# Scratch reads from another queue, polled searches, an earlier load of a norm weight and two new pacing rates in a two-block transformer kernel

## The chip, the cores and the metric

The kernel runs on one core of one Trainium2 chip. The metric is the device time of one execution in microseconds, the median of three runs. One profiled execution of the same kernel gives the rows below.

## What is computed

A 256-token sequence of width 2048 goes through two blocks. The first one mixes by convolution and neighbourhood attention and ends in an MLP; the second mixes by latent attention and a gated unit and ends in a layer of 16384 experts (PEER), of which every token uses 8 heads times 16 experts. The change lies wholly in that last layer:

```python
def peer_ffn(h, w_pq, peer_keys, peer_u, peer_v):
    q = jnp.einsum("bsd,dhk->bshk", h, w_pq).reshape(B, S, PEER_HEADS, 2, KEY_DIM)
    sub = jnp.einsum("bshpk,hpnk->bshpn", q, peer_keys).astype(jnp.float32)
    s, i = lax.top_k(sub, PEER_TOPK)
    cand = (s[..., 0, :, None] + s[..., 1, None, :]).reshape(B, S, PEER_HEADS, PEER_TOPK * PEER_TOPK)
    cidx = (i[..., 0, :, None] * N_KEYS + i[..., 1, None, :]).reshape(...)
    top_s, pos = lax.top_k(cand, PEER_TOPK)
    idx = jnp.take_along_axis(cidx, pos, axis=-1)
    gate = jax.nn.softmax(top_s, axis=-1).astype(h.dtype)
    ...
        u = jnp.take(peer_u, i_blk, axis=0)
        a = jax.nn.gelu(jnp.einsum("td,thkd->thk", x_blk, u)) * g_blk
        v = jnp.take(peer_v, i_blk, axis=0)
        return jnp.einsum("thk,thkd->td", a, v)
```

The kernel computes 192 of the 256 tokens densely: it multiplies them with all 16384 rows of `peer_u`, applies GELU, multiplies by a gate that is zero for the experts not chosen, and multiplies with all of `peer_v`. The other 64 tokens are done sparsely: only the chosen rows are gathered.

## The kernel before, in words

All large products go through one pipeline. A weight tile of 128x2048 floats (1 MB) is loaded by SyncE into one of three `raw` buffers; a piece is half of it, 128x1024. `prep` splits a piece into two roundings: ScalarE writes `whi` (L131), VectorE writes the remainder `wlo` (L132), and TensorE multiplies with both (L264). There are four `whi`/`wlo` pairs, and pieces are prepared up to three ahead (`LOOK = 3`). When the second half of a `raw` tile has been split, SyncE is given the load of the tile three further on (L209). SyncE's queue holds nothing else in this part.

All other work is written as generators. `tick` is called after each piece and advances each generator in the list by its rate: 1.0 means one step per piece, 0.45 means 0.45 steps per piece. A generator that is started in a piece skips the tick of that piece. `drain` runs a generator to its end at once, so that all that is left of it is put into the engines' queues in one burst. Engines work their queues in order, so the order in which the generators are stepped is the order of VectorE.

The stages of the last layer, with the generators of each:

- Query groups (four, eight pieces each). After group n `key_gen(n)` makes the scores `sub` in five steps, and `lists_gen(n)` (L1485 to L1489) polls until the scores are there and then makes eight searches, one per step: the 16 best of 128 scores for one head and half.
- `U0` to `U3`: passes over `peer_u`, each of four groups of eight pieces, so 32 pieces. After each group `turn(n)` transposes the result into a ring (GELU). `turn(8)` first drains `top_gen`.
- `top_gen` starts with the last query group. It drains all `key_gen` and `lists_gen`, then makes the best 16 of the 256 sums for each head (L1525 and again L1485 on 256 elements) and the gates. It has 57 steps after the waiting, at one per piece.
- `g_gen` (rate 0.5, 25 steps) follows it: it builds the dense gates with one-hot products and writes them to a DRAM scratch in 24 writes (L1690, GpSimd's queue). At its end it starts `sparse`.
- `r_gen(e)`, e from 0 to 7: after the last `turn` of U pass e, after `g_gen` and after `r_gen(e-1)`, it reads the gates of pass e back from the scratch in three reads of 512 KB (L1698, GpSimd's queue, one buffer `t`), and multiplies the ring with each (L1703, VectorE). In step j the read is issued; two ticks later comes the multiply.
- `sparse` (rate 0.45 in U passes, 0.28 in V passes, set by `pace`): the first step loads the norm's weight `g_n2` broadcast over 128 partitions (1 MB, GpSimd's queue), multiplies the 64 tokens with it (L1591) and copies the product to the other partitions (L1592, GpSimd's queue). The second issues three gathers (L1598, GpSimd's queue) and computes the first; each of the 128 steps gathers 128 rows (1 MB) into one of three buffers, and VectorE multiplies and reduces them (L1608, `peer_u`) or adds them up (L1610, `peer_v`).
- `V` passes over `peer_v`: 32 pieces each. Before each second piece `jit_V` splits two columns of the ring (`s_vj`), and before the first piece of a pass it drains `top_gen`, `g_gen` and the `r_gen` of that pass. `jit_V` runs two pieces ahead.

The order of passes is U0 U1 U2 U3 V0 U4 V1 U5 V2 U6 V3 U7 and then V4 to V7 as one pass of 128 pieces. In the trace U3 ends and V0 begins at 2302.7 us; U4 lies from 2401.5 to 2480.2, V1 to 2576.0, U5 to 2654.6, V2 to 2744.1, U6 to 2822.7, V3 to 2916.3, U7 to 2995.0, and the last pass to 3329.

Of the kernel before, what the change touches and what calls it, by code (L numbers as in the profile page):

```python
# [12 lines left out]
OP = mybir.AluOpType  # L13
# [925 lines left out]

GATE_RATE = 0.5  # L940

SPARSE_RATE = (0.45, 0.28)
CONV_RATE = [1.7, 1.2]
NA_RATE = [1.0, 1.0]
CONV_POOL = (2, 3, 6, 7)
# [2 lines left out]
def phase3(b, C, W, gs, X, ident, transposes, residual, norm_of, stat2, act_pair, lhs_of, res_need, bcast, jits,  # L948
# [546 lines left out]

    def lists_gen(n):
        V16, I16, _, rep = found()
        while not gs["key", n].done:
            yield
        for h in range(2):  # L1500
            for m in range(4 * n, 4 * n + 4):
                o = (h * 16 + m) * 16
                top16(V16[:, o:o + 16], I16[:, o:o + 16], SUB(h)[:, m * 128:m * 128 + 128], rep[m % 2][:, :128])
                yield

    def top_gen():
        V16, I16, If, rep = found()
        for n in range(4):
            gs["key", n].drain()
            gs["lists", n].drain()  # L1510
        V.tensor_copy(If, I16)
        yield
        t8 = H(8, "sub")
        T16 = t8[:, 0:128]
        Pi, Pa, Pb = (t8[:, k * 128:k * 128 + 128].bitcast(U32) for k in (1, 2, 3))
        Fa, Fb, E = t8[:, 512:640], t8[:, 640:768], t8[:, 768:1152]
        sm = t8[:, 1152:1160]
        cand, eq = H(16, "k")[:, :], H(17, "k")[:, :]
        i1, i2, g12, it2 = sarr16()
        V.tensor_copy(it2, iota[:, :, None].to_broadcast([128, 128, 2]))  # L1520
        for h in range(2):
            v4 = V16[:, h * 256:h * 256 + 256].rearrange("p (m q k) -> p m q k", m=8, q=2)
            f4 = If[:, h * 256:h * 256 + 256].rearrange("p (m q k) -> p m q k", m=8, q=2)
            for m in (0, 4):
                V.tensor_tensor(cand[:, m * 256:m * 256 + 1024].rearrange("p (m a c) -> p m a c", m=4, a=16),  # L1525
                                v4[:, m:m + 4, 0, :, None].to_broadcast([128, 4, 16, 16]),
                                v4[:, m:m + 4, 1, None, :].to_broadcast([128, 4, 16, 16]), op=OP.add)
                yield
            for m in range(8):
                top16(T16[:, m * 16:m * 16 + 16], Pi[:, m * 16:m * 16 + 16], cand[:, m * 256:m * 256 + 256],  # L1530
                      rep[m % 2])
                yield
            V.tensor_scalar(Pa, Pi, 4, None, op0=OP.logical_shift_right)
            V.tensor_scalar(Pb, Pi, 15, None, op0=OP.bitwise_and)
            V.tensor_copy(Fa, Pa)
            V.tensor_copy(Fb, Pb)
            yield
            for q, F in enumerate((Fa, Fb)):
                for m in (0, 4):
                    e1 = eq[:, m * 256:m * 256 + 1024]  # L1540
                    e3 = e1.rearrange("p (s a) -> p s a", a=16)
                    e4 = e1.rearrange("p (m s a) -> p m s a", m=4, s=16)
                    V.tensor_tensor(e3, F[:, m * 16:m * 16 + 64, None].to_broadcast([128, 64, 16]),
                                    iota[:, None, 0:16].to_broadcast([128, 64, 16]), op=OP.is_equal)
                    yield
                    V.tensor_tensor(e4, e4, f4[:, m:m + 4, q, None, :].to_broadcast([128, 4, 16, 16]), op=OP.mult)
                    yield
                    V.tensor_reduce(E[:, q * 128 + m * 16:q * 128 + m * 16 + 64], e3, axis=AX.X, op=OP.add)
                    yield
            g = E[:, 256:384].rearrange("p (m s) -> p m s", m=8)  # L1550
            t3 = T16.rearrange("p (m s) -> p m s", m=8)
            V.tensor_tensor(g, t3, t3[:, :, 0:1].to_broadcast([128, 8, 16]), op=OP.subtract)
            A.activation(g, g, AF.Exp)
            V.tensor_reduce(sm, g, axis=AX.X, op=OP.add)
            V.reciprocal(sm, sm)
            V.tensor_tensor(g, g, sm[:, :, None].to_broadcast([128, 8, 16]), op=OP.mult)
            if h:
                t = t8[:, 1160:1288].bitcast(I32)
                V.scalar_tensor_tensor(t, E[:, 0:128], 128.0, E[:, 128:256], op0=OP.mult, op1=OP.add)
                V.tensor_copy(which[64:128], t[64:128, 0:64])  # L1560
                V.tensor_copy(share[64:128], E[64:128, 256:320])
                nc.gpsimd.dma_start(which[0:64], t[64:128, 64:128])
                nc.gpsimd.dma_start(share[0:64], E[64:128, 320:384])
            for _ in range(4):
                yield
            p = b.bank()
            for k in range(3):
                PE.transpose(p[:, k * 128:k * 128 + 128], E[:, k * 128:k * 128 + 128], ident)
            s = slice(h * 128, h * 128 + 128)
            V.tensor_copy(i1[:, s], p[:, 0:128])  # L1570
            V.tensor_copy(i2[:, s], p[:, 128:256])
            V.tensor_scalar(g12[:, 0, s], p[:, 256:384], GSCALE, None, op0=OP.mult)
            V.scalar_tensor_tensor(g12[:, 1, s], p[:, 256:384], GSCALE, g12[:, 0, s], op0=OP.mult, op1=OP.subtract)
            yield
        gs["G"] = b.start(g_gen(), GATE_RATE)


# [6 lines left out]
    def sparse():  # L1584
        xs = H(8, "sp")[:, :]
        buf = [H(5, "gb")[:, :], H(16, "k")[:, :], H(17, "k")[:, :]]
        hi, lo = slice(64, 128), slice(0, 64)
        nc.gpsimd.dma_start(buf[2], bcast("g_n2"))
        A.activation(Y()[hi], X[1][hi], AF.Copy)
        G.memset(Y()[lo], 0.0)  # L1590
        V.tensor_tensor(xs[hi], X[1][hi], buf[2][hi], op=OP.mult)  # L1591
        nc.gpsimd.dma_start(xs[lo], xs[hi])  # L1592
        G.memset(X[1][hi], 0.0)
        yield

        def load(g):
            at = bass.IndirectOffsetOnAxis(ap=which[:, g % 64:g % 64 + 1], axis=0)
            nc.gpsimd.indirect_dma_start(buf[g % 3], None, d["v_rows" if g // 64 else "u_rows"], at)  # L1598

        def gelu(a, z):  # L1600
            A.activation(act[:, a:z], act[:, a:z], AF.Gelu_apprx_tanh, scale=rsp)
            V.tensor_tensor(act[:, a:z], act[:, a:z], share[:, a:z], op=OP.mult)
        for g in range(3):
            load(g)
        for g in range(128):
            t, a = buf[g % 3], act[:, g % 64:g % 64 + 1]
            if g < 64:
                V.tensor_tensor_reduce(t, t, xs, 1.0, 0.0, OP.mult, OP.add, a)  # L1608
            else:
                V.scalar_tensor_tensor(Y(), t, a, Y(), op0=OP.mult, op1=OP.add)  # L1610
            if g + 3 < 128:
                load(g + 3)
            if g in (32, 64):
                gelu(g - 32, g)
            yield
# [42 lines left out]
    def g_gen():  # L1658


        i1, i2, g12, it2 = sarr16()
        i1, i2, g1, g2 = (a.rearrange("p (k u t) -> p k u t", u=4, t=2) for a in (i1, i2, g12[:, 0], g12[:, 1]))
        numbers = it2[:, None, :, :].to_broadcast([128, 4, 128, 2])
        room = [H(5, "gb"), H(17, "k")]
        out = [H(16, "k")[:, i * 1024:i * 1024 + 1024] for i in range(2)]
# [27 lines left out]
    def r_gen(e):  # L1693
        while not (gs["s", 4 * e + 3].done and "G" in gs and gs["G"].done and (e == 0 or gs["R", e - 1].done)):
            yield
        t = H(7, "g")[:, 1024:2048]
        for j in range(3):
            nc.gpsimd.dma_start(t.rearrange("p (k m) -> p k m", k=8),  # L1698
                                b.scratch[8 * j:8 * j + 8, :, 128 * e:128 * e + 128].rearrange("k p m -> p k m"))
            yield  # L1700
            yield
            R = ring(e, j // 2)[:, :, j % 2 * 64:j % 2 * 64 + 64].rearrange("p n (k t) -> p k n t", k=8)
            V.tensor_tensor(R, R, t.rearrange("p (k n t) -> p k n t", k=8, n=16), op=OP.mult)  # L1703
            yield
# [32 lines left out]
    def post_V(last, g):  # L1737
        def f(p, halves=(0, 1), blocks=(0, 1)):
# [3 lines left out]
            for h in halves:  # L1742
                for k in blocks:
                    s = slice((2 * g + k) * 512, (2 * g + k) * 512 + 512)
                    V.tensor_tensor(X[h][:, s], X[h][:, s], b.ps[p.banks[h][k]][:, :], op=OP.add)  # L1745
                    if last and h == 0:
                        A.activation(b.bank()[:, :], X[h][:, s], AF.Square,  # L1747
                                     accum_out=ssf[:, h, 2 * g + k:2 * g + k + 1])
                    elif last and g:
                        gs["gain"].drain()  # L1750
                        join(2 * g + k)
            if last and g and 1 in blocks:
# [168 lines left out]
```

## Time and profile before

| | us |
|---|---|
| median of three runs | 3346.87 |
| lowest, highest | 3342.87, 3348.78 |
| the profiled execution, its own time | 3345.87 |
| span of its trace, first to last instruction | 3344.1 |
| TensorE busy | 3185.3 (95%) |
| VectorE busy | 2271.5 (68%) |
| ScalarE busy | 1728.1 (52%) |
| GpSimd busy | 505.3 (15%) |

Busy is the time in which an engine works an instruction. The granted clock is the share of TensorE's full clock (2.4 GHz) that it was allowed, so 0.5 is 1.2 GHz. The share of the DMA is the mean busy share of the core's 16 DMA engines.

### The profile page before, as it was taken

The numbers are of one execution on the slowest core, as the hardware profiler recorded it, in microseconds if no ns is written. First come the engines' busy times: TensorE is split into PE (matmuls) and PEld (weight loads), VectorE is DVE, ScalarE is ACT, GpSimd is POOL, SyncE is SP. The second block draws the span as 40 slices with busy tenths as digits, with TensorE's granted clock in tenths as the row PEclk, the third lists the DMA queues.
The fourth block names the chain that finished last, engine by engine and source line by source line (L and its number), as shares of the span: only waits on it lengthen the run. The fifth ranks groups of instructions, "written<-read, shape, count | busy, mean of one in ns | idle before, by whom it ended". The sixth has DMA issues, their size and how long they took to land. (4 is left out here: it accounts for less than half of the span.)

```text
span 3344.1 us, 37944 instructions
## 1 busy us (share of the span) xinstructions
PE 3185.3 (95%) x14264; PEld 2485.6 (74%) x14264; DVE 2271.5 (68%) x2847; ACT 1728.1 (52%) x2490; POOL 505.3 (15%) x397
## 2 busy tenths in 40 slices
PE   8899999999999999999999989997999989898998
PEld 6577778888888798877778867775676767675776
DVE  6995544444555656544555799867878888886885
ACT  5666454444454465455445445763454545454554
POOL 3861100000000100000002000013222222332210
PEclk9899999999999999999999999998999999998999
DMA  6444455555555455444455445778898989797984
GB/s 220 142 165 170 171 191 186 177 178 187 189 189 189 156 177 212 178 147 141 169 180 184 170 165 211 255 257 331 325 368 315 403 310 396 282 411 270 351 323 151
DMA packets 113736, 768.52 MB, mean 230 GB/s; under 512 B 13008, under 2 KB 13440, under 8 KB 26064
## 3 DMA queue, kind: packets, MB, share of 16 engines
q1 hardware_dynamic: 84960, 591.70, 48.7%
q0 software_dynamic: 28304, 173.36, 13.5%
q8 instruction: 111, 1.82, 0.2%
q10 hardware_dynamic: 288, 1.05, 0.1%
q14 instruction: 73, 0.60, 0.1%
HBM read 750.82 MB, written 14.68 MB: 229 GB/s over the span
## 5 line engine op out<-in xcount | busy, mean ns | idle before, releaser
L132 DVE TENSOR_TENSOR wlo<-raw,whi 128x1024 fp32r<-128x1024 f32 (+2 forms) x1101 | 1350.8, 1235 | 797.6 <-ACT whi L131 790.2
L131 ACT ACTIVATE whi<-raw 128x1024 fp32r<-128x1024 f32 (+2 forms) x1113 | 1168.4, 1053 | 1117.0 <-PE ps L264 956.0
L264 PE MATMUL ps<-whi,s_x 128*128 128x512 f32 (+2 forms) x2816 | 907.8, 398 | 11.7 <-ACT whi L131 6.3
L264 PEld LDWEIGHTS ps<-whi,s_x 128*128 128x128 f32 x2816 | 532.8, 190 | 138.1 <-issue 8.3
L264 PE MATMUL ps<-whi,s_h 128*128 128x512 f32 x1760 | 609.2, 403 | 0.0
L264 PE MATMUL ps<-whi,s_vj 128*128 128x512 f32 x1536 | 549.6, 413 | 28.2 <-DVE s_vj L132 24.9
L264 PE MATMUL ps<-wlo,s_x 128*128 128x512 f32 (+2 forms) x1408 | 555.4, 394 | 13.0 <-DVE wlo L132 13.0
L264 PE MATMUL ps<-wlo,s_h 128*128 128x512 f32 (+1 forms) x1136 | 454.3, 400 | 34.9 <-DVE wlo L132 34.9
L264 PE MATMUL ps<-wlo,s_vj 128*128 128x512 f32 (+1 forms) x1024 | 416.3, 407 | 40.1 <-DVE wlo L132 40.1
L264 PEld LDWEIGHTS ps<-whi,s_h 128*128 128x128 f32 x1760 | 334.9, 190 | 101.3 <-issue 1.4
L264 PEld LDWEIGHTS ps<-whi,s_vj 128*128 128x128 f32 x1536 | 299.2, 196 | 140.6 <-DVE s_vj L132 36.9
L264 PE MATMUL ps<-whi,s_fj 128*128 128x512 f32 x1024 | 324.4, 397 | 2.8 <-DVE s_fj L132 2.0
L264 PEld LDWEIGHTS ps<-wlo,s_x 128*128 128x128 f32 x1408 | 267.3, 190 | 77.3 <-DVE wlo L132 21.4
L264 PEld LDWEIGHTS ps<-wlo,s_h 128*128 128x128 f32 (+1 forms) x1136 | 187.9, 165 | 88.2 <-DVE wlo L132 41.2
L264 PEld LDWEIGHTS ps<-wlo,s_vj 128*128 128x128 f32 (+1 forms) x1024 | 170.9, 167 | 92.1 <-DVE wlo L132 44.7
L264 PEld LDWEIGHTS ps<-whi,s_fj 128*128 128x128 f32 x1024 | 193.5, 189 | 51.4 <-DVE s_fj L132 2.5
L264 PE MATMUL ps<-wlo,s_fj 128*128 128x512 f32 x512 | 203.6, 398 | 0.0
L132 POOL TENSOR_TENSOR s_head<-raw,s_head 128x1024 fp32r<-128x1024 f32 x6 | 17.5, 2932 | 896.0 <-ACT s_head L131 896.0
L517 POOL TENSOR_TENSOR s_conv<-s_conv,s_u 128x256 f32<-128x256 f32 x120 | 125.6, 1080 | 43.1 <-ACT s_u L516 42.8
L1598 POOL DMA_INDIRECT s_k<-in_v_rows,vec x43 | 81.6, 1897 | 244.4 <-DVE s_sp L1610 224.5
L264 PEld LDWEIGHTS ps<-wlo,s_fj 128*128 128x128 f32 x512 | 96.8, 189 | 22.7
L1598 POOL DMA_INDIRECT s_k<-in_u_rows,vec x42 | 69.9, 1664 | 214.5 <-DVE misc L1608 210.7
(335 smaller groups left out, 3039.3 us busy)
## 6 DMA issues: line engine op xcount, KB each, us to landing
raw<-in_peer_u SPq DMA_DIRECT2D x128, 1024.0 KB, 5.8
raw<-in_peer_v SPq DMA_DIRECT2D x128, 1024.0 KB, 6.8
raw<-in_w_in SPq DMA_DIRECT2D x101, 1024.0 KB, 4.8
raw<-in_w_up SPq DMA_DIRECT2D x64, 1024.0 KB, 4.8
raw<-in_w_down SPq DMA_DIRECT2D x64, 1024.0 KB, 4.8
raw<-in_w_out SPq DMA_DIRECT2D x32, 1024.0 KB, 4.8
raw<-in_w_pq SPq DMA_DIRECT2D x16, 1024.0 KB, 4.8
scratch<-s_k POOLq DMA_DIRECT2D x24, 512.0 KB, 3.8
```

The costliest lines, as they stand in the source:

```text
L131: nc.scalar.activation(hi, src, AF.Copy)
L132: (engine or nc.vector).tensor_tensor(lo, src, hi.bitcast(FT), op=OP.subtract)
L264: nc.tensor.matmul(self.ps[p.banks[h][b]][:xs[q].shape[-1], :w], xs[q], (wl if q == 1 else wh)[:, s], start=p.first and c == 0 and q == 0, ...
L517: G.tensor_tensor(o, o, t, op=OP.add)
L1598: nc.gpsimd.indirect_dma_start(buf[g % 3], None, d["v_rows" if g // 64 else "u_rows"], at)
```

## The change

The scratch reads of `r_gen` are issued by SyncE in place of GpSimd, and one more step lies between a read and its multiply. `lists_gen(n)` begins only after `lists_gen(n-1)` is done, and `top_gen` polls for the last of them instead of draining them. The load of `g_n2` moves from the start of `sparse` to the start of `g_gen`, into another buffer (`Y`); the copy in the setup of `sparse` goes to SyncE, the first three gathers are issued in its first step, and the clearing work forms a step of its own, so that the first gathered rows are used in the third step. The rates of `sparse` rise from 0.45 to 0.48 and from 0.28 to 0.30. The end of the last pass drains `sparse` before it drains the generator of the final gain.

```diff
-SPARSE_RATE = (0.45, 0.28)
+SPARSE_RATE = (0.48, 0.30)
...
-        while not gs["key", n].done:
+        while not (gs["key", n].done and (n == 0 or gs["lists", n - 1].done)):
             yield
...
-        for n in range(4):
-            gs["key", n].drain()
-            gs["lists", n].drain()
+        while not gs["lists", 3].done:
+            yield
         V.tensor_copy(If, I16)
...
-        nc.gpsimd.dma_start(buf[2], bcast("g_n2"))
-        A.activation(Y()[hi], X[1][hi], AF.Copy)
-        G.memset(Y()[lo], 0.0)
-        V.tensor_tensor(xs[hi], X[1][hi], buf[2][hi], op=OP.mult)
-        nc.gpsimd.dma_start(xs[lo], xs[hi])
-        G.memset(X[1][hi], 0.0)
-        yield
+        V.tensor_tensor(xs[hi], X[1][hi], Y()[hi], op=OP.mult)
+        nc.sync.dma_start(xs[lo], xs[hi])
...
         for g in range(3):
             load(g)
+        yield
+        A.activation(Y()[hi], X[1][hi], AF.Copy)
+        G.memset(Y()[lo], 0.0)
+        G.memset(X[1][hi], 0.0)
+        yield
...
+        nc.gpsimd.dma_start(Y(), bcast("g_n2"))
         numbers = it2[:, None, :, :].to_broadcast([128, 4, 128, 2])
...
-            nc.gpsimd.dma_start(t.rearrange("p (k m) -> p k m", k=8),
-                                b.scratch[8 * j:8 * j + 8, :, 128 * e:128 * e + 128].rearrange("k p m -> p k m"))
+            nc.sync.dma_start(t.rearrange("p (k m) -> p k m", k=8),
+                              b.scratch[8 * j:8 * j + 8, :, 128 * e:128 * e + 128].rearrange("k p m -> p k m"))
+            yield
             yield
             yield
...
+                        gs["sp"].drain()
                         gs["gain"].drain()
```

## Rows read from the trace of the kernel before

**Rows 1.** The page's part 1: busy time, share of the span, instructions of each engine.
```profile
PE 3185.3 (95%) x14264; PEld 2485.6 (74%) x14264; DVE 2271.5 (68%) x2847; ACT 1728.1 (52%) x2490; POOL 505.3 (15%) x397
```

**Rows 2.** Busy time by stretches: length, engines' busy us (instructions), clock, DMA share, GB/s.
```profile
1913.00:1970.00 57.00, 40.85 (x176) 29.76 (x175) 54.80 (x190) 20.74 (x24) 0.00 (x0) 0.88 0.32 111
2244.00:2302.70 58.70, 40.01 (x148) 28.59 (x148) 35.61 (x31) 16.88 (x21) 18.17 (x16) 0.85 0.81 302
2302.70:2401.50 98.80, 84.82 (x333) 61.12 (x332) 78.27 (x96) 42.90 (x67) 22.15 (x16) 0.91 0.86 320
2480.20:2576.00 95.80, 82.40 (x334) 60.72 (x333) 71.63 (x91) 43.01 (x67) 18.18 (x12) 0.91 0.79 304
2654.60:2744.10 89.50, 80.51 (x334) 59.71 (x333) 72.78 (x91) 42.73 (x67) 18.99 (x13) 0.94 0.83 322
2822.70:2916.30 93.60, 81.17 (x333) 60.12 (x332) 71.20 (x79) 43.00 (x66) 31.29 (x12) 0.93 0.82 309
2995.00:3060.00 65.00, 49.12 (x183) 35.60 (x182) 39.01 (x42) 23.89 (x38) 15.82 (x8) 0.84 0.66 249
3060.00:3165.00 105.00, 105.00 (x452) 79.77 (x451) 93.98 (x105) 58.90 (x89) 23.51 (x13) 1.00 0.92 356
```

**Rows 3.** The same view for U4, one of four like passes.
```profile
2401.50:2480.20 78.70, 78.70 (x358) 60.61 (x357) 71.85 (x66) 40.78 (x47) 23.73 (x14) 1.00 0.97 395
```

**Rows 4.** Who waited for whom: total us, times, longest.
```profile
PE ps L264 <- DVE wlo L132: 88.1, 38, 12.5
DVE s_ra L1703 <- DMA s_g<-scratch: 62.0, 12, 11.7
DVE s_rc L1703 <- DMA s_g<-scratch: 38.3, 7, 8.6
DVE s_sp L1591 <- DMA s_k<-in_g_n: 9.8, 1, 9.8
```

**Rows 5.** Instructions in order: start, us, engine, operation [idle before]; VectorE at the searches.
```profile
1912.40 1.22 DVE L132 TENSOR_TENSOR wlo<-raw,whi 128x1024 fp32r<-128x1024 f32 x1 [0.27 <-ACT whi L131]
...
1915.12 0.27 DVE L1485 MAX8 s_top<-s_sub 128x8 f32<-128x128 f32 x1
...
1932.38 0.28 DVE L1485 MAX8 s_top<-s_sub 128x8 f32<-128x128 f32 x1
...
1934.41 1.22 DVE L132 TENSOR_TENSOR wlo<-raw,whi 128x1024 fp32r<-128x1024 f32 x1
...
1940.29 0.42 DVE L1485 MAX8 s_sub<-s_k 128x8 f32<-128x256 f32 x1
...
1943.66 0.42 DVE L1485 MAX8 s_sub<-s_k 128x8 f32<-128x256 f32 x1
```

**Rows 6.** The same view, TensorE after the searches.
```profile
1935.68 0.79 PE L264 MATMUL ps<-wlo,s_h 128*128 128x512 f32 x1 [12.51 <-DVE wlo L132]
```

**Rows 7.** The same view at V1's first scratch read: GpSimd, then VectorE.
```profile
2488.42 1.68 POOL L1598 DMA_INDIRECT s_gb<-in_u_rows,vec  x1 [5.86 <-DVE misc L1608]
2490.09 0.96 POOL L1698 DMA_DIRECT2D s_g<-scratch  x1
...
2505.33 1.23 DVE L1703 TENSOR_TENSOR s_ra<-s_ra,s_g 128x1024 f32<-128x1024 f32 x1 [11.67 <-DMA s_g<-scratch]
```

**Rows 8.** The same view at the start of the sparse part: GpSimd, then VectorE.
```profile
2268.39 0.97 POOL L1698 DMA_DIRECT2D s_g<-scratch  x1
...
2264.13 2.29 DVE L1608 CUSTOM_DVE_ANT_0 s_gb<-s_gb,s_sp 128x2048 f32<-128x2048 f32 x1 [6.86 <-DMA s_gb<-in_u_rows,vec]
...
2277.44 1.22 DVE L1703 TENSOR_TENSOR s_rc<-s_rc,s_g 128x1024 f32<-128x1024 f32 x1 [5.38 <-DMA s_g<-scratch]
```

**Rows 9.** The view by tile, scratch from 2480 to 3060: issue to landing.
```profile
DMA to landing us min/median/max: 4.9/8.6/15.2
```

**Rows 10.** Busy time in 4 us after one wait in V1.
```profile
2512.00:2516.00 4.00, 4.00 (x11) 2.89 (x10) 0.71 (x1) 1.27 (x2) 0.83 (x1) 0.50 0.97 340
```

**Rows 11.** DMA issues from 2480 to 3060: count, KB each, median us to landing.
```profile
raw<-in_peer_v SPq DMA_DIRECT2D x56, 1024.0 KB, 7.4
```

**Rows 12.** DMA issues in U4: the same columns.
```profile
raw<-in_peer_u SPq DMA_DIRECT2D x12, 1024.0 KB, 9.7
```

## The prediction

> **What bounds the kernel now.** I read the busy shares first: TensorE works 95% of the span [rows 1], so only its gaps can be won. The table by stretches then shows where they are: U4 has none (78.70 busy of 78.70) [rows 3], nor has the last pass once it is under way (105.00 of 105.00) [rows 2]; the gaps lie in the first pieces of U0, at the change from U3 to V0 and at the start of every V pass. Each such stretch also has a granted clock below 1.00 [rows 2], and a slice right after a wait stood at 0.50, which is 1.2 GHz, with TensorE busy all through and 11 matmuls in 4 us [rows 10]; so a gap costs more than its idle time.
>
> I therefore price a stretch by its length less what its work takes without gaps. A matmul in the undisturbed part of the last pass takes 105/452 = 0.232 us. A piece is ten, so 2.33 us including rounding; 32 pieces are 74.3 us. U4 has 4.3 us more for its four turns, so a V pass, which holds one turn, would take 75.4. What is lost:
> - searches: 57.0 - 176 x 78.7/358 = 18.3 us;
> - start of the sparse part: 58.7 - 148 x 0.220 = 26.2, and V0: 98.8 - 75.4 = 23.4, together 49.6;
> - V1, V2, V3: 20.4, 14.1, 18.2, and the first 65 us of the last pass: 65 - 183 x 0.232 = 22.5, together 75.2 [rows 2, 3].
>
> In all 143 us, the ceiling of this change. The table of waits says why: TensorE waits for VectorE's `wlo`, and VectorE waits 100 us for the scratch reads (19 times) and 9.8 for `g_n2` [rows 4].
>
> **Searches.** Steps counted from the last query group's piece as 0: before, `top_gen` drains in piece 1, where four searches of list 2 and eight of list 3 are left. They stand in a row, 1.57 us each (1915.12 to 1932.38 is eleven steps) [rows 5], and the next `wlo` comes 22 us after the one before; TensorE stands 12.5 us [rows 6]. After: the lists were already one search per piece (`lists_gen(n)` takes eight pieces and the next begins as it ends), so the chaining itself does nothing; polling in place of draining spreads the twelve over pieces 2 to 13. A piece then asks VectorE for 1.14 + 1.57 = 2.7 us against 2.46 of TensorE in a U pass [rows 3, 5], 0.25 short for 13 pieces, and after that eight searches over 256 elements make a step of 3.37 us (1940.29 to 1943.66) [rows 5], 0.9 short each. The sum is 10.5 us short, less three prepared pieces, 7 us. I leave 3 us, bounds 0 and 8: **gain 15**.
>
> **What the polling moves.** `top_gen` begins at piece 14 instead of 1, and all behind it shifts by 13: it ends at piece 71 (before `turn(8)` would drain it at 73), `g_gen` at 122 instead of 109. V0's first piece is number 129, and its `jit_V` runs before piece 127's products. `r_gen(0)` issues its first read at 123, multiplies at 126 (three ticks), and is then drained with two reads left. That is a new burst: two times landing plus multiply, one after the other, on VectorE, with two pieces (4.7 us) ready. Landings at this place with gathers running were 9.0 (2268.39 to 2277.44) [rows 8]; the shortest later one was 4.9 and the median 8.6 [rows 9]. Two at 4.9 give 2 x (4.9 + 1.2) + 0.7 - 4.7 = 8 us of standstill, two at 9.0 give 16; gathers have just been issued, but the queue is not yet full, so I take 14, with 3 for the slow clock after it.
>
> **Start of the sparse part and V0.** What goes: VectorE's 9.8 us for `g_n2` [rows 4] and 6.9 for the first gather [rows 8]. The load now has `g_gen`'s 50 pieces, over 120 us, to land; uncovered it would cost the 9.8 again. The gathers are issued two steps before use, over four pieces, which with the drain covers the 6.9. The copy on SyncE waits for a 2.3 us multiply, with the weight loads queued behind it; SyncE's next load has five pieces before it is split, so I put it at nothing (at worst 2.3). `r_gen(1)` to `r_gen(3)` follow with nine reads, at 1 us each. So 14 + 3 + 9 = 26 stay of the 49.6: **gain 24**, bounds 8 and 40.
>
> **The reads of V1 to V4.** Why they are late: in V1 the first is issued behind a gather that waited 5.9 us for VectorE, 1.7 us after it, lands 15.2 us later, and VectorE stands 11.7 us [rows 7]. On SyncE it has no gather in front of it, neither in the engine's queue nor in the DMA queue that GpSimd's transfers share. SyncE gets there when the `wlo` of that piece is done, some 3 to 4 us earlier than GpSimd did here, and the multiply stands one piece (2.33 us) later. Of the 11.7 that leaves 5 to 6 if the landing stays 15, nothing if it is the 8.6 of the median. In exchange it stands behind weight loads, whose median landing is 7.4 here [rows 11] and 9.7 in U4 [rows 12], and the load after it stands behind it. A weight load is issued five pieces (11.7 us) before its first half is due for splitting and TensorE needs that some two pieces after, so it may land about 14 us after its issue, an estimate from the piece time; against 7.4 that is 6.6 us of cover, more than a read's 512 KB take at half of 395 GB/s (2.7 us). I leave 3 us for the first read of each group and 1 for the other two, 20 in all, and 2 for the clock: of 75.2, 22 stay, **gain 53**; bounds 5 left and 45 left.
>
> How a read of 512-byte runs fares on SyncE's queue no row shows; its range is the 4.9 to 15.2 of the landings on GpSimd's [rows 9], and I take the lower half, since the weight loads on that queue land in 7.4 [rows 11].
>
> **Rates.** A U pass at 0.48 makes 15.4 gathers of 1.05 MB instead of 14.4, in all 32.9 MB with the sixteen weight tiles. U4 ran at 395 GB/s with a DMA share of 0.97 [rows 3], so the full share is 407 GB/s and the pass would need 80.8 us for 78.7: up to 2.1 us in each of four passes, nothing if the three buffers carry it into the V pass. I take 1 each, **a loss of 4**, bounds 0 and 9. VectorE has room (71.85 of 78.70, plus one step of 2.3). In V passes 0.02 x 32 steps of 2.3 us are 1.5 us on an engine that is not full. The sparse part now has 130 steps, of which 102 are done at the last pass, and ends at its piece 93 of 128 (98 before), so the new drain finds it done: nothing.
>
> **Sum.** 15 + 24 + 53 - 4 = 88; the profiled execution's 3345.9 becomes 3258. The median of the runs lies 1 us above it: **3259**.
>
> **The rivals.**
> - *The move alone buys only the issue.* The reads keep their landing times, because the DMA engines are full, and each wait shrinks by the added piece and the shorter issue, some 2.9 us. Then, over the 19 waits, about 53 of the 100 us remain: 40 stay of the 75 instead of 22, and 5 more in V0: 3282. For it: the DMA share of 0.97 in the U pass before each V pass [rows 3]. Against: the late issue behind the gather [rows 7]. The Trainium skill, "DMA: Bandwidth & Descriptors", section "Issuing engines are not separate DMA queues", says that: DMAs of any engine run on the same 16 DMA engines, and another issuing engine saves only sequencer time. No row here shows a read on SyncE.
> - *The late gates.* The drain before V0 also meets the three first gathers and the copy: both landings near 15, so 2 x (15.2 + 1.2) + 0.7 - 4.7 = 29 us instead of 14, and `r_gen(1)` to `r_gen(3)`, now inside V0, stay late: the 49.6 stay whole. 3283. For it: the order of steps is sure, only the landings are not. Against: the longest landing stands at a pass that began with full queues.
> - *Slower: the reads hold up the weights.* On SyncE's queue a read of short runs delays each weight tile behind it. From a delay of 6.6 us TensorE pays; 21 reads (those after the drain) with a delay of 15.2, the longest landing [rows 9], cost 21 x 8.6 = 181 us, and 3259 + 181 = 3440. From 11 us a read on, 21 x 4.4 = 92 eats the gain. Against: the reads move half of what a weight tile moves.
>
> The same skill page, "Queues, rings and completion order", states that descriptors of a ring are consumed in order, which is what this rival needs; that alone sets no price.
>
> **How the numbers follow.** The forecast has 0.66, the first rival 0.18, the second 0.12, the slower one 0.03; 0.01 is left for no change. The range: the low end takes 3 less in the searches, 14 less in V0 and 14 less in the reads, 3228; the high end takes the first rival with the rates' full 9 and half of the second, 3300. About 0.2% (7 us) is what this kernel's runs can tell from no change, so faster is 0.96, same 0.01, slower 0.03.
>
> **What would show it.** No search burst and a TensorE gap under 5 us near 1935; one gap of 10 to 20 us just before V0, with two scratch waits on VectorE in a row; no wait for `g_n2` or the first gather; VectorE's waits for scratch under 50 us in all; U passes at 78.7 to 80 us; V1 to V3 near 80 us. It is wrong if V passes stay above 88, if ScalarE waits for weight tiles at their start, or if the U passes grow past 81.

## The result and the profile after

The change makes the kernel faster, by less than forecast: 3288.11 us in the median of four runs (3283.24 to 3295.18) against 3346.06 us for the kernel before on the same chip. The ratio is 0.9829, 95% interval 0.9809 to 0.9849. That is 58 us, where 88 were forecast. The profiled execution took 3288.91 us, its span 3287.1 us, so the two spans differ by 57.0 us, and rows of the two traces can be set side by side.

I read the page's part 1 of after first, and set it beside [rows 1]:

```profile
PE 3164.6 (96%) x14264; PEld 2474.4 (75%) x14264; DVE 2271.0 (69%) x2847; ACT 1725.9 (53%) x2490; POOL 480.5 (15%) x372
```

TensorE does the same 14264 matmuls in 20.7 us less busy time (less of it at a lowered clock), so 36 of the 57 us are idle time that went. Where it went, the busy time by stretches of after tells; the columns are those of [rows 2]. In order: the searches, the last pieces before V0, V0, U4, V1, U5, V2, V3 and the first 65 us of the last pass.

```profile
1930.00:1990.00 60.00, 58.53 (x267) 44.45 (x266) 58.45 (x154) 31.76 (x36) 0.00 (x0) 1.00 0.53 183
2225.00:2281.80 56.80, 36.93 (x224) 28.41 (x222) 28.38 (x28) 24.93 (x27) 8.97 (x9) 0.86 0.75 269
2281.80:2377.00 95.20, 84.25 (x332) 62.02 (x333) 75.99 (x93) 45.34 (x69) 16.92 (x10) 0.91 0.82 294
2377.00:2459.60 82.60, 79.57 (x357) 60.16 (x357) 74.46 (x67) 38.82 (x46) 23.52 (x14) 1.00 0.99 392
2459.60:2547.00 87.40, 80.55 (x333) 60.38 (x333) 77.15 (x97) 44.34 (x68) 17.84 (x11) 0.94 0.93 353
2547.00:2625.70 78.70, 78.70 (x358) 60.58 (x358) 72.34 (x68) 40.59 (x47) 25.22 (x15) 1.00 0.99 399
2625.70:2710.90 85.20, 78.55 (x333) 58.78 (x332) 74.30 (x91) 43.19 (x66) 16.06 (x10) 0.98 0.92 353
2789.60:2874.30 84.70, 78.54 (x333) 58.70 (x332) 73.70 (x79) 43.50 (x67) 21.30 (x10) 0.98 0.94 353
2953.00:3018.00 65.00, 60.39 (x256) 44.98 (x255) 57.36 (x63) 34.78 (x54) 16.92 (x8) 0.97 0.95 361
```

Against [rows 2, 3]: the search stretch now runs at clock 1.00 with TensorE nearly always busy, 58.53 of 60.00. The stretch before V0 still has 20 us of nothing. V0 is hardly shorter (95.2 for 98.8) and still at a clock of 0.91. U4, which had no gap, has grown from 78.7 to 82.6. V1 to V3 have lost 4 to 9 us each, and the last pass now does 256 matmuls in its first 65 us, where it did 183.

Every pass is priced the same way below, in this and in the other kernels, from TensorE's first matmul with a pass's operand to the next pass's first one. "Q, U0-3" begins with the first query group; U5, U6 and U7 stayed at 78.6 to 80.2 throughout and are left out; with them a row makes that kernel's span less about 1824 us. e3 has no row, since its profiled execution was a slow one (4394.04 us).

| kernel (what it is) | Q, U0-3 | V0 | U4 | V1 | V2 | V3 | last |
|---|---|---|---|---|---|---|---|
| before | 478.9 | 98.8 | 78.7 | 95.8 | 89.4 | 93.6 | 349.1 |
| after | 457.0 | 95.2 | 82.6 | 87.4 | 85.2 | 84.8 | 334.1 |
| e1 (after, old rates) | 457.0 | 94.6 | 81.1 | 85.2 | 82.0 | 80.6 | 329.6 |
| e2 (before + reads) | 463.9 | 85.1 | 79.9 | 82.3 | 82.5 | 82.2 | 333.1 |
| e4 (before + polling) | 448.4 | 124.8 | 78.7 | 94.3 | 85.0 | 95.8 | 340.9 |
| e5 (after, gates at 0.7) | 462.4 | 92.8 | 78.7 | 83.9 | 84.0 | 82.9 | 329.9 |
| e6 (e1, gates at 0.7) | 455.2 | 94.7 | 80.3 | 84.3 | 81.5 | 83.6 | 328.0 |
| e7 (before + rates) | 485.3 | 128.9 | 78.7 | 95.8 | 95.5 | 94.7 | 349.4 |
| e8 (before + sparse start) | 470.2 | 99.1 | 78.6 | 96.5 | 89.1 | 93.1 | 348.1 |
| e9 (e2 + polling, gates at 0.7) | 454.4 | 93.0 | 80.7 | 84.2 | 84.0 | 90.2 | 326.5 |
| e10 (e6, gathers later) | 448.7 | 92.8 | 79.6 | 89.9 | 83.9 | 83.1 | 328.9 |
| e11 (e2, two more steps) | 461.3 | 79.7 | 84.3 | 77.1 | 76.9 | 76.3 | 325.5 |
| e12 (e6, two more steps) | 446.5 | 81.8 | 85.0 | 76.9 | 77.3 | 77.9 | 325.0 |

**The searches** came out as said. TensorE's waits between 1925 and 1990 us, in order (start, us, operation, idle before it and what ended it), are three short ones where [rows 6] had one of 12.51:

```profile
1973.33 0.51 PE L264 MATMUL ps<-wlo,s_h 128*128 128x512 f32 x1 [0.38 <-DVE wlo L132]
1976.70 0.50 PE L264 MATMUL ps<-wlo,s_h 128*128 128x512 f32 x1 [0.33 <-DVE wlo L132]
1983.44 0.50 PE L264 MATMUL ps<-wlo,s_h 128*128 128x512 f32 x1 [0.76 <-DVE wlo L132]
```

With two more of 0.78 at 2052 they make 3 us, the 3 that the forecast left.

**The gap before V0** is the one that was foretold, but longer. These are GpSimd, SyncE, VectorE and TensorE there, in the same kind of view:

```profile
2250.87 1.03 POOL L1592 DMA_INDIRECT s_gb<-in_u_rows,vec  x1 [0.33 <-DMA scratch<-s_k]
2254.12 1.46 POOL L1592 DMA_INDIRECT s_k<-in_u_rows,vec  x1 [2.21 <-DVE wlo L132]
2255.89 1.99 POOL L1592 DMA_INDIRECT s_k<-in_u_rows,vec  x1 [0.30 <-issue]
...
2252.79 0.38 SPq L1698 DMA_DIRECT2D s_g<-scratch  x1
...
2271.03 0.53 SPq L1588 DMA_DIRECT2D s_sp<-s_sp  x1
2272.23 0.34 SPq L209 DMA_DIRECT2D raw<-in_peer_v  x1
2272.87 14.06 SPq L1698 DMA_DIRECT2D s_g<-scratch  x3
...
2267.40 1.23 DVE L1704 TENSOR_TENSOR s_ra<-s_ra,s_g 128x1024 f32<-128x1024 f32 x1 [10.34 <-DMA s_g<-scratch]
2268.66 2.29 DVE L1587 TENSOR_TENSOR s_sp<-s_x,s_sp 64x2048 f32<-64x2048 f32 x1
2270.98 1.23 DVE L132 TENSOR_TENSOR wlo<-raw,whi 128x1024 fp32r<-128x1024 f32 x1
2280.14 1.23 DVE L1704 TENSOR_TENSOR s_ra<-s_ra,s_g 128x1024 f32<-128x1024 f32 x1 [7.93 <-DMA s_g<-scratch]
2285.32 1.23 DVE L1704 TENSOR_TENSOR s_rc<-s_rc,s_g 128x1024 f32<-128x1024 f32 x1 [3.96 <-DMA s_g<-scratch]
...
2281.87 0.80 PE L264 MATMUL ps<-whi,s_vj 128*128 128x512 f32 x1 [19.94 <-ACT s_vj L131]
```

The forecast had two waits in a row, after the first read's own multiply. There are three. The first read is issued at 2252.79, among three gathers of 1 MB that GpSimd issued at 2250.87, 2254.12 and 2255.89. `sparse` starts some pieces after the read in the code, but GpSimd had almost nothing to wait for (0.33 us), so the first gather went ahead of it. The read takes 14.6 us to land, VectorE waits 10.34, and TensorE stands 19.94. That the gathers make it late, e6 and e10 below show: the same read lands in 14.9 us beside them and in 6.2 ahead of them.

The second read shows another cost. Its buffer is free when the first multiply ends at 2268.63, but on SyncE a weight load (L209) stands before it, and that waits for the `wlo` that VectorE makes until 2272.21, behind the multiply of L1587. So the second read leaves 4.2 us later, at 2272.87. The copy of L1588 stands before both, but it had left at 2271.03, ahead of that `wlo`, and held up neither.

**Who waited for whom**, over the whole span, with the columns of [rows 4]:

```profile
DVE s_ra L1704 <- DMA s_g<-scratch: 41.0, 13, 10.3
DVE s_rc L1704 <- DMA s_g<-scratch: 16.2, 7, 4.0
PE ps L264 <- DVE s_vj L132: 35.8, 20, 3.9
PE ps L264 <- DVE wlo L132: 22.4, 25, 2.1
PE ps L264 <- ACT s_vj L131: 19.9, 1, 19.9
```

VectorE's waits for the scratch fell from 100.3 to 57.2 us, TensorE's for `wlo` from 88.1 to 22.4. What TensorE waits for now is `s_vj`, the split columns of the ring, which stand behind the late multiply.

### The profile page after: what moved, and what is told of

Same layout as the page of the kernel before. It is cut to its first block, busy times and chain, and to the rows that moved or that the text cites. A ratio compares the mean times of both kernels' runs of the same rounds, so it can differ in the third digit from the quotient of the medians.

```text
span 3287.1 us, 37918 instructions
## 1 busy us (share of the span) xinstructions
PE 3164.6 (96%) x14264; PEld 2474.4 (75%) x14264; DVE 2271.0 (69%) x2847; ACT 1725.9 (53%) x2490; POOL 480.5 (15%) x372
## 5 line engine op out<-in xcount | busy, mean ns | idle before, releaser
L264 PE MATMUL ps<-whi,s_vj 128*128 128x512 f32 x1536 | 542.7, 408 | 59.2 <-DVE s_vj L132 35.8
L264 PEld LDWEIGHTS ps<-wlo,s_x 128*128 128x128 f32 x1408 | 267.9, 190 | 80.7 <-DVE wlo L132 24.3
L1592 POOL DMA_INDIRECT s_k<-in_v_rows,vec x43 | 91.3, 2123 | 201.7 <-DVE s_sp L1609 179.7
L1609 DVE SCALAR_TENSOR_TENSOR s_sp<-s_k,misc,s_sp 128x2048 f32<-128x2048 f32 x43 | 100.8, 2345 | 2.1 <-DMA s_k<-in_v_rows,vec 2.1
```

The costliest lines, as they stand in the source:

```text
L264: nc.tensor.matmul(self.ps[p.banks[h][b]][:xs[q].shape[-1], :w], xs[q], (wl if q == 1 else wh)[:, s], start=p.first and c == 0 and q == 0, ...
```

## The experiments

Each kernel was timed beside the kernel before, on the same chip; a ratio is that of the two, with its 95% interval.

**My theory** after the result: the reads, not the rest, make the gain; the new rates take a part of it in the V passes; the gates end late and leave a drain before V0. The rivals: the extra step alone makes the gain and the queue none; polling or the sparse start carry it; SyncE's queue is what is left to pay.

### Undoing one part, adding one part

**e1_rates_back**: after, with the old rates.

```diff
-SPARSE_RATE = (0.48, 0.30)
+SPARSE_RATE = (0.45, 0.28)
```

> The changed kernel with the two rates put back to 0.45 and 0.28. Theory: the higher rates cost the 3.9 us that U4 lost and keep the DMA queues fuller when the scratch reads of a V pass are issued, so VectorE's waits for scratch (57 us in the changed kernel) fall and the time is 3276 to 3284 instead of 3288. Rival: the V passes are as late with either rate, since the reads stand behind the weight loads of their own queue; then only U4 comes back and the time is 3284 to 3290.

Measured: 3271.97 us, 0.9790 (0.9772 to 0.9807), better than after and beyond the theory. By the ratios the rates cost 13 us, by the medians 16, against 4 in the forecast. The table of passes has it in U4 (1.5) and in V1, V2, V3 and the last (2.2, 3.2, 4.2, 4.5). ScalarE's waits for weight tiles, from 2450 us to the end, in after:

```profile
ACT whi L131 <- DMA raw<-in_peer_u: 47.5, 23, 3.5
ACT whi L131 <- DMA raw<-in_peer_v: 45.3, 26, 5.2
```

and in e1:

```profile
ACT whi L131 <- DMA raw<-in_peer_v: 36.4, 21, 4.0
ACT whi L131 <- DMA raw<-in_peer_u: 29.3, 15, 3.4
```

27 us more of ScalarE's waiting, while VectorE's waits for the scratch reads of that part are the same (21.1 us from V1 on in after, 20.9 in e1). So the rates don't cost by making the reads later. That they cost by late weight tiles is not shown: 11 of the 27 us lie in V1 to V3 and the last pass and 13 in U5 to U7, where TensorE has no gap; V2, 3.2 us longer in after, has fewer of them there (3.4 against 7.2); and in after TensorE's gaps in V1 to V3 all stand before matmuls that wait for VectorE's `s_vj`. Of the 14 us some 8 are idle time of TensorE, the rest its work at a lower clock (0.94 in V1, where e1 has 0.98).

**e2_reads_only**: before, with the reads on SyncE and the added step.

```diff
-            nc.gpsimd.dma_start(t.rearrange("p (k m) -> p k m", k=8),
+            nc.sync.dma_start(t.rearrange("p (k m) -> p k m", k=8),
...
+            yield
```

> The kernel before with nothing but the scratch reads moved to SyncE and the added step between read and multiply. Theory: this is all of what V1 to V4 gained (36 us) and a part of V0's, so 3300 to 3312 against 3346. Rival: the gain comes from the whole (fewer gathers waiting in GpSimd's queue, the sparse part's changed start), then 3318 to 3330.

Measured: 3266.29 us, 0.9766 (0.9749 to 0.9784), 77 us below before: more than the whole change, and more than either expectation. V0 falls from 98.8 to 85.1, V1 from 95.8 to 82.3. VectorE's waits for the scratch are down to

```profile
DVE s_ra L1704 <- DMA s_g<-scratch: 20.1, 9, 4.4
DVE s_rc L1704 <- DMA s_g<-scratch: 8.5, 4, 3.3
```

28.6 us, half of what they are in after. With the gates at their old place no gap stands at V0: the one wait of TensorE over 0.4 us between 2240 and 2300 us is the 9.09 behind the first gather, for which VectorE waits 12.19.

**e3_step_only**: before, with the added step alone, the reads still on GpSimd (only the `yield` of e2).

> The kernel before with nothing but the added step; the reads stay on GpSimd. Theory: the late issue behind a gather is the larger part of the waits, so the step alone gives at most half of what the kernel with both gives: 3322 to 3334. Rival: the queue is of no account and the longer cover does it all: the same as with both, 3300 to 3312.

Measured: 3313.16 us, 0.9908 (0.9890 to 0.9925), 30 us below before and between the two ranges. That is less than half of e2: the other 47 us come with the queue. The rival that the step alone makes the gain falls.

**e4_polling_only**: before, with chained lists and polling.

```diff
-        while not gs["key", n].done:
+        while not (gs["key", n].done and (n == 0 or gs["lists", n - 1].done)):
...
-        for n in range(4):
-            gs["key", n].drain()
-            gs["lists", n].drain()
+        while not gs["lists", 3].done:
+            yield
```

> The kernel before with nothing but the polled and chained searches. Theory: the gap of 12.5 us after the searches goes (17 us with the slow clock), and the gates, which end 13 pieces later, put two scratch reads into a drain before V0 that gives some 10 us back: 3334 to 3342. Rival one: no give-back, 3327 to 3331. Rival two: the drain takes all of it, 3344 to 3350.

Measured: 3329.60 us, 0.9959 (0.9944 to 0.9973), 14 us below before. The number is that of the first rival, but not for its reason, that nothing is given back. The passes show a trade: query groups and U0 to U3 win 30.5 us, V0 loses 26.0. Moving the gates back frees the searches and brings the first reads to the edge of V0 (issued from 2253.94 to 2276.42, where V0 begins at 2276.62) and the first gathers into it (2285.68).

### The sparse start, the rates alone, earlier gates

**e5_gates_faster**: after, with the gates' generator made faster, so that it ends some twenty pieces before V0.

```diff
-GATE_RATE = 0.5
+GATE_RATE = 0.7
```

> The changed kernel with the gates' generator at 0.7 steps per piece instead of 0.5, so that it ends at piece 108 instead of 122 and the three reads for V0 are through at piece 121, before the drain at 127. Theory: the 19.9 us gap before V0 is that drain and goes with its slow clock: 3262 to 3270 instead of 3288. Rival: VectorE has no room for the gates at this pace (3.0 us per piece in U2 and U3) or the reads are late there anyhow: 3280 to 3290.

Measured: 3275.19 us, 0.9792 (0.9776 to 0.9808), 0.0037 or 12 us better than after, between the two expectations. V0 is 92.8 instead of 95.2: an earlier end of the gates takes little out of it. What is won lies behind it, 3.9 us in U4 and 10.8 from V1 on, and 5.4 are lost ahead of it, in the query groups and U0 to U3 (457.0 to 462.4).

**e6_gates_faster_rates_back**: e5 with the rates of e1.

> The changed kernel with the gates at 0.7 and the two rates of the sparse part back at 0.45 and 0.28. Theory: the drain (20 to 24) and the rates (14) are separate losses and add up: 3248 to 3256. Rival: they overlap, since less is left for the sparse part to catch up with once it starts earlier: 3258 to 3266.

Measured: 3269.85 us, 0.9775 (0.9759 to 0.9792). The two gains do not add: 5 us better than e5, and the same as e1 within the intervals. The theory fell here, and the rival's range was missed too. The passes say more of the rates: with the gates at 0.7, V1 to V3 and the last pass take 580.7 us at the new rates (e5) and 577.4 at the old ones, while the query groups and U0 to U3 take 462.4 and 455.2. So the 14 us that the rates cost the V passes in after are 3.3 here. In the trace the first read, issued at 2220.53 us, lands 14.9 us later, VectorE waits 12.21 and TensorE 9.49: the gap has moved with the start of the sparse part instead of closing.

**e7_rates_only**: before, with the new rates and the drain at the end.

```diff
-SPARSE_RATE = (0.45, 0.28)
+SPARSE_RATE = (0.48, 0.30)
...
+                        gs["sp"].drain()
                         gs["gain"].drain()
```

> The kernel before with nothing but the two rates (and the drain at the end, without which the generator of the gain could not finish). Theory: the rates cost by themselves, through fuller DMA queues and VectorE's place in the V passes: 4 to 14 us more than the 3344 of the kernel before, 3348 to 3358. Rival: they cost only beside reads on SyncE, where weight tiles and reads share a queue: 3340 to 3347.

Measured: 3390.84 us, 1.0139 (1.0122 to 1.0156), 48 us slower than before: the sign was right, the size far off. V0 alone grows by 30.1 us. GpSimd and then VectorE in V0 of e7:

```profile
2330.41 1.70 POOL L1598 DMA_INDIRECT s_k<-in_u_rows,vec  x1 [13.45 <-DVE misc L1608]
2332.10 0.96 POOL L1698 DMA_DIRECT2D s_g<-scratch  x1
2346.58 1.71 POOL L1598 DMA_INDIRECT s_k<-in_u_rows,vec  x1 [13.53 <-DVE misc L1608]
2348.28 0.96 POOL L1698 DMA_DIRECT2D s_g<-scratch  x1
...
2342.87 1.23 DVE L1703 TENSOR_TENSOR s_ra<-s_ra,s_g 128x1024 f32<-128x1024 f32 x1 [8.26 <-DMA s_g<-scratch]
2344.02 2.28 DVE L1608 CUSTOM_DVE_ANT_0 s_k<-s_k,s_sp 128x2048 f32<-128x2048 f32 x1
...
2358.50 1.22 DVE L1703 TENSOR_TENSOR s_rc<-s_rc,s_g 128x1024 f32<-128x1024 f32 x1 [8.25 <-DMA s_g<-scratch]
```

The two generators run in lockstep. The gather waits some 13 us for the sparse product (L1608), the read stands right behind the gather on GpSimd, VectorE stands 8.3 us for the read, and only behind that multiply is the next sparse product made, for which the next gather waits. Six turns of this, 13 to 17 us each, lie between 2314 and 2408 us, the first and the last of them weaker (the first gather waits 5.09 us, the last read costs VectorE 3.17). This is [rows 7] six times in a row. Before, some reads in V0 were issued clear of a gather; the new rate moves the sparse steps against the reads. VectorE's waits for the scratch are 137.8 us in all (84.8 and 53.0) against 100.3.

**e8_sparse_start_only**: before, with the new start of the sparse part (the earlier load of `g_n2`, the copy on SyncE, the gathers two steps ahead).

> The kernel before with nothing but the new start of the sparse part: weight of the norm loaded with the gates, copy on SyncE, gathers in the first step. Theory: VectorE's 9.8 and 6.9 us of waiting go and TensorE's gaps of 7.3 and 4.9 us with them: 3328 to 3336. Rival: the scratch reads that follow take the place of these waits: 3339 to 3345.

Measured: 3334.74 us, 0.9975 (0.9964 to 0.9986), 8.4 us below before, as the theory had it; 8.7 of it stand in the query and U passes, the only part that it touches.

The four parts alone make -77.3, +47.7, -14.0 and -8.4 us, together -52, near the -58 of the whole. This nearness says little, since the parts do not add: the rates cost 48 us alone, 16 in after and 5 between e5 and e6, and in e4 and e7 single passes move by 26 to 30 us.

### What still stands: queue, gathers or cover

**e9_reads_polling_gates**: e2 with the polling of e4 and the gates at 0.7, old sparse start and old rates.

> The kernel before with the reads on SyncE (and their added step), the polled searches and the gates at 0.7; the sparse part starts as before and at the old rates. Theory: the new start, with its three gathers ahead of the first scratch read, only trades one wait for another (the read then lands 14.6 us after its issue), so without it the parts add up: 3266 less 14, 3249 to 3257. Rival: the old start's own waits for the norm's weight and the first gather cost as much: 3262 to 3270, like the changed kernel with gates at 0.7 and old rates.

Measured: 3276.14 us, 0.9797 (0.9776 to 0.9818), 10 us above e2. Both expectations missed. The passes show the polling's gain in the query and U passes (463.9 to 454.4) and its loss in V0 (85.1 to 93.0) and V3 (82.2 to 90.2); VectorE's waits for the scratch are 50.3 us instead of 28.6. The longest of these waits stands in V3: a read issued at 2790.42 lands 14.30 us later, and VectorE waits 7.99 for it (4.37 for its counterpart in e2). Why these two passes and not V1 and V2, no run settles.

**e10_gathers_after_clearing**: e6, with the first three gathers issued after the clearing work, one step later.

```diff
-        for g in range(3):
-            load(g)
         yield
...
         G.memset(X[1][hi], 0.0)
+        for g in range(3):
+            load(g)
         yield
```

> The changed kernel with the gates at 0.7, the old rates, and the first three gathers issued behind the clearing work of the second step, which waits for VectorE's multiply, instead of in the first step, where GpSimd waits for nothing and is ahead of the scratch read. Theory: the first read lands in 5 to 8 us instead of 15, the 9.5 us gap of TensorE in U3 goes: 3254 to 3262 against 3270. Rival: the gathers then hit the second read and VectorE's first use of them, and the gap only moves: 3266 to 3272.

Measured: 3267.39 us, 0.9775 (0.9755 to 0.9794), the ratio of e6. The first half of the theory holds: the first read lands in 6.23 us instead of 14.93, and VectorE waits 3.52 for it instead of 12.21. But the rival has the time: TensorE's gap of 9.49 is one of 7.04 us, at 2247.55, behind the second read and VectorE's 3.87 us for the first gather. The passes win 6.5 us ahead of V0 and 1.9 in it and lose 5.6 in V1, where a read lands in 14.71. The order of gathers and first read is worth 2 to 3 us of gap and nothing in the time.

**e11_reads_more_cover**: e2, with five steps in place of three between a read and its multiply.

```diff
+            yield
+            yield
             yield
             yield
             yield
```

> The kernel with the moved reads only, with five steps between a read and its multiply instead of three. Theory: what is left in the V passes (82.3 us against 75.4) is VectorE waiting 2 to 4 us for a read that lands in 8 to 10 us, with the two columns for the next piece behind it; 4.7 us more cover takes that away, V passes of 77 to 79 us and 3244 to 3256 against 3266. Rival: the V passes are held by weight tiles that land late beside gathers and reads: V passes stay above 81 and the time at 3262 to 3268.

Measured: 3247.07 us, 0.9718 (0.9699 to 0.9738), as the theory had it; the rivals, that SyncE's queue or the weight tiles hold V1 to V3, fall. V1 to V3 take 76.3 to 77.1 us, where 75.4 was the forecast's price without gaps. VectorE's waits for the reads in the whole span, and the time from issue to landing of all 48 scratch transfers (24 of them reads; the view by tile):

```profile
DVE s_ra L1706 <- DMA s_g<-scratch: 1.0, 2, 0.5
...
DMA to landing us min/median/max: 3.1/6.3/16.0
```

A landing of 16 us, in U4, is still there, longer than any in [rows 9], and VectorE waits 0.54 us for it. What stays open is in V0 and U4, at a full DMA:

```profile
2286.30:2366.00 79.70, 77.23 (x334) 57.59 (x332) 75.15 (x92) 44.05 (x68) 15.12 (x9) 1.00 0.99 377
2366.00:2450.30 84.30, 80.38 (x358) 61.75 (x357) 76.80 (x71) 40.57 (x48) 21.34 (x15) 0.98 1.01 399
```

**e12_all_more_cover**: after, with all that was learnt.

```diff
-GATE_RATE = 0.5
+GATE_RATE = 0.7
...
-SPARSE_RATE = (0.48, 0.30)
+SPARSE_RATE = (0.45, 0.28)
...
             yield
             yield
             yield
+            yield
+            yield
```

> The changed kernel with the gates at 0.7, the old rates, and five steps between a scratch read and its multiply instead of three. Theory: short cover, not the queue, is what is left in the V passes and in front of V0, and with it gone the searches (15 us) and the sparse part's start (9) come on top of the kernel with moved reads and five steps (3247): 3224 to 3236, with V passes of 76 to 78 us and no wait for scratch over 4 us on VectorE. Rival: polling moves the twelve reads of the first passes to where the gathers begin, and the weight tiles of V0 and U4 are late instead: 3240 to 3252.

Measured: 3230.32 us (3229.51 to 3233.64), 0.9665 (0.9648 to 0.9681): 112 us below before and 58 below after (55 by the ratios), the best of all. The first read is issued 1.6 us behind the first gather here too, but TensorE waits 2.61 us at the most between 2200 us and V0, and the waits of VectorE for the scratch are

```profile
DVE s_ra L1706 <- DMA s_g<-scratch: 10.8, 2, 7.7
```

The 7.7 is that first read, landing in 15.16 us, so the "no wait over 4 us" of the theory was missed. Against e11 it wins 17 us, nearly all of it in the query and U passes (461.3 to 446.5). So the gain of the searches, which e9 lost again, stays in the kernel whose reads have cover.

## Why the prediction was right, and where its sizes were off

The time fell inside the range, on the side forecast, but 29 us above the value. Its terms, each beside what the passes of before, e1 and after give:

| term | forecast | measured | from |
|---|---|---|---|
| searches | +15 | +15 | 18.3 lost before, 3.0 of gaps after |
| start of the sparse part and V0 | +24 | +11 | Q, U0-3 and V0: 577.7 to 551.6 in e1, less 15 |
| reads in V1 to V4 | +53 | +50.5 | V1 to V3 and last: 627.9 to 577.4 in e1 |
| U4, old rates | 0 | -2.4 | 78.7 to 81.1 in e1 |
| rates | -4 | -16 | after less e1, by passes and by medians |

The measured column makes 58. Two terms were mis-sized, and they make 25 of the 30 us that are missing.

**The rates.** The step that failed is "In V passes 0.02 x 32 steps of 2.3 us are 1.5 us on an engine that is not full". It priced the rates by VectorE's time in V passes, at nothing, and by the DMA's only in U passes. The runs show 14 of the 16 us in V passes (after and e1). What carries them there stays open. The V passes of after run at a DMA share of 0.92 to 0.94, where before had 0.79 to 0.83 [rows 2], but e1 has 0.92 to 0.94 too, at the old rates, and e5 has 0.93 to 0.95 at the new ones, where V passes pay 3.3 us. U5 to U7, where I had put the loss, stayed at 78.6 to 78.7; U4 at 82.6 is beyond the 81 that I had named as a sign of error, and of its 3.9 us only 1.5 are the rates'. Beside the rest stand reads of `r_gen(3)` that ran over into it (VectorE waits 4.11 us for one at 2378.96) and late weight tiles; no run tells them apart.

**The start of the sparse part and V0.** Forecast to stay: 14 for the gap, 3 for the clock, 9 for `r_gen(1)` to `r_gen(3)`. Measured: 19.94 for the gap; V0's idle time is 95.20 - 84.25 = 11.0; its matmuls take 84.25 - 75.4 = 8.9 more than at the full clock. So the gap is 6 us too small, the clock 6 and the reads 2. The gap: I had the first read wait for nothing, with the gathers issued behind it. They were issued around it, it landed in 14.6, and a weight load that waited for its `wlo` held the second read back by 4.2 us, which no term of the sum had. The copy on SyncE, put "at nothing (at worst 2.3)", was no part of that. The shape of the "late gates" rival is what came, with the first landing long (14.6) and the second not (7.3): its gap of 29 us was 19.94. The clock: granted 0.91 over V0, not 1.00 less a moment. I had let one gap cost 3 us, but V0 has several: besides the 19.94, waits of 2.99, 3.94, 1.78, 0.86 and 1.22 us.

**The reads** were sized well (53 against 50.5), yet not for all the reasons given. The step "nothing if it is the 8.6 of the median" failed: reads of that landing still waited. From the old place, 2480 to 3060 us, ten of the twelve reads cost VectorE 73.8 us; in after, the twelve from V1 on cost 21.1. (The "20 in all" of the forecast are time of TensorE, so the two can't be set side by side.) But the landing has not changed. These are the twelve reads of the V1 to V4 groups in after, the counterpart of [rows 9]:

```profile
DMA to landing us min/median/max: 6.5/8.5/13.0
```

The median was 8.6. So the first rival was right about the DMA, and wrong about what the move buys. It priced the earlier issue at the added piece and the shorter issue, 2.9 us for each wait; the reads of V1 to V4 gained 52.7 us on ten waits, 5.3 each. The row that told of it was [rows 7], a read that stood on GpSimd's queue behind a gather which waited 5.86 us for VectorE. In the trace of before the eight second and third reads of V1 to V4 left 0.3 to 7.6 us after their buffer was free, 3.3 in the mean; in that of after each left 1.54 us after it. e3 and e2 size both: 30 us for the step, 47 more for the other queue. That the gather's wait is all of the 47 is argued, from these rows and the equal landings; no run separates it from the rest that goes with another queue. That its total, 3282, lies nearer to the result than mine, and its 53 us of VectorE's waits near the measured 57.2, is two errors that cancel, since 36 of the 57 lie ahead of V1, in the drain (18.3) and in V0 and U4 (17.8).

The Trainium skill, "DMA: Bandwidth & Descriptors", section "Issuing engines are not separate DMA queues", says that transfers of all engines share the 16 DMA engines and that another issuing engine saves only time on the sequencer, usually a small one. This case agrees with the first half, by 8.5 against 8.6 us of landing. Of "usually small" it is an exception: away from a sequencer that is held by gathers' waits, the move was worth 47 us (e3 to e2).

**The slower rival** (reads hold up the weights) didn't come. The median landing of the `peer_v` tiles over the whole span is 7.0 us, 6.8 before; e2, with reads on SyncE alone, is 77 us faster.

**What the forecast said should be seen**: no search burst (so it is); one gap of 10 to 20 us before V0 (19.94) with two scratch waits in a row (three); no wait for `g_n2` or for the first gather (none); VectorE's scratch waits under 50 us (57.2, by the 18.3 of the drain); V1 to V3 near 80 (84.8 to 87.4 with the new rates, 80.6 to 85.2 in e1). Of its three signs of being wrong two came: U4 at 82.6, and ScalarE's waits for weight tiles at the start of V1 (2.96 and 2.26 us) and of the last pass (3.42 and 2.44). The third did not: no V pass from V1 on is above 88.

What stays open: why polling costs V0 and V3 but not V1 and V2 in e9, what makes the rates dear with late gates and nearly free in V passes with early ones, what five steps of cover would give on the old queue, and what the 5 to 6 us are that U4 keeps in e11 and e12, at a DMA share of 0.99 to 1.01. No run took U4's weight tiles or gathers apart.

## What to carry to other kernels

Give a transfer enough cover, in steps between issue and use, beside choosing the queue that it is issued on: on the new queue two more steps (e11) closed what neither an earlier issue nor another order could, and made the landing time itself nearly harmless. An instruction that stands behind a gather on its queue shares the gather's wait, so look for a transfer that is issued right after a long idle of its own engine. Price a pacing rate in every pass that it touches, and measure it again after each other change, since its price moved from 48 us to 16 and 5. Ask which drain a generator that is moved later will run into.

## What the runs showed of the hardware

The same read is cut in another way on SyncE's queue. The totals of packets on the page of before and, below, of after:

```profile
DMA packets 113736, 768.52 MB, mean 230 GB/s; under 512 B 13008, under 2 KB 13440, under 8 KB 26064
```

```profile
DMA packets 135240, 768.52 MB, mean 234 GB/s; under 512 B 13008, under 2 KB 38016, under 8 KB 47568
```

e2, which moves nothing but the reads, has the numbers of after. Between 512 bytes and 2 KB there are 24576 more, 1024 for each of the 24 reads of 512 KB, so 512 bytes each; between 2 and 8 KB there are 3072 fewer, 128 of 4 KB for each read. I had left open how runs of 512 bytes fare there. They land as before (8.5 us against 8.6), so packets eight times smaller cost nothing that these rows show. The Trainium skill, "DMA: Bandwidth & Descriptors", section "Specifications", puts the smallest transfer at full rate at 512 bytes; no scratch read here went below it.

A change of 7% in the pace of one generator cost 48 us on the old queue (e7) and 16 on the new one, or 5, hardly clear of the noise, with earlier gates (e5 to e6). Two streams that meet on one in-order queue can lock into step, and how they meet is set by rates that look harmless.
